# Hybrid backbone block: the first modulation with the weights stationary and two conditioning columns moving

## The chip, the cores and the metric

The kernel runs on one core of one Trainium2 chip. The time is that of the device, in microseconds, for one execution of the whole program. A run is compared by the median of several executions of the kernel before on the same chip.

## What is computed

One block of a flow-matching generator: 2048 latent tokens and 256 context tokens of width 1024. Everything is modulated by a vector computed from the conditioning `c` (for latent tokens) and `c_ctx` (for context tokens). The part that matters here:

```python
mod = jax.nn.silu(c) @ w_ada[l] + b_ada[l]          # 1024 -> 6 * 1024
mod_c = jax.nn.silu(c_ctx) @ w_ada[l] + b_ada[l]
sh1, sc1, g1, sh2, sc2, g2 = ...                     # six parts of 1024 each
q_c, k_c, v_c, p_c, gt_c = _split_proj(_modulate(ctx, csh1, csc1) @ w_in[l])
q, k, v, p, gt = _split_proj(_modulate(x, sh1, sc1) @ w_in[l])
```

`_modulate(z, shift, scale)` is the normalised z times (1 + scale) plus shift. After that come windowed attention with context keys, a pooling branch, gates, an output projection, a layer norm and a two-layer MLP. Only the first two parts of the modulation (shift and scale of the first sub-layer, 2048 of the 6144 columns of `w_ada`) are needed for both `c` and `c_ctx`, and they are needed first. The other four parts are computed much later in the program by another routine, on VectorE.

## The kernel before, in words

All products are made at the precision of float32. A plain float32 matmul of this kernel appears in the trace as two records of a matmul, each with a weight load of its own. The large products instead split each operand into a high and a low part (`split`, L57 to 62) and use three matmuls.

**The start.** The first 92 us or so are one stage, written as straight code (L127 to 400), whose order on each engine is set when the program is built by a scheduler with a model of the time line. From L401 on, the attention's order on TensorE is written out by hand.

**The first modulation.** The vector silu(c), silu(c_ctx) is built on ScalarE and VectorE as `cs`, 128 partitions x 8 k-tiles x 2 columns (L202 to 206). `csw` (L207, L208) widens it: each of the two columns is repeated 64 times, so that one k-tile of it is a full 128x128 stationary operand. `ada_load(c)` (L146) loads 512 columns of `w_ada` as four tiles `adaw` of 512 KB, two k-tiles each, and `ada_use(c, ws)` (L156) computes with them. There are four such chunks: 0 and 1 are the shift, 2 and 3 the scale; 0 and 2 serve the first half of the width, 1 and 3 the second. In `ada_use` eight float32 matmuls with `csw` as the stationary operand and 512 moving columns of weights make one PSUM bank `ps_ada` (L159), whose rows are 64 copies of either result. ScalarE copies it to `row` (L161), four transposes through TensorE bring the 512 columns onto partitions (`ps_adat`, L164), and VectorE picks one of the 64 copies, adds the bias and writes `mod` (L166); for chunks 2 and 3 it adds 1 (L168). `ps_ada` has the tag `proj`, of which there is one bank: the next chunk's first matmul waits until that bank has been read. The same bank later holds the q products.

**What follows in the start.** Two context blocks (xc) and two latent blocks (x01) are normalised on VectorE (L214), transposed (`ps_u`, L230), scaled by `mod` (L235 on ScalarE, L237 on VectorE), split (L240, L247) and multiplied by the k and v columns of `w_in` (`ps_ckv`, `ps_kv`, L252 to 254): the first half of the width after chunks 0 and 2, the second half after chunks 1 and 3. `wq_load(k)` (L176) loads the q columns, 8 times 512 KB through two buffers `wraw` (L179), and splits each on ScalarE (high) and on GpSimd (low; VectorE for the last two). `q_units` multiplies the blocks by them (`ps_q`).

**Buffers and queues.** The tiles `adaw`, `csw` and `wq` share two rings, a0 and a1, of eight buffers each, taken in program order: `csw` is the seventh tile of a0, the first `wq` the eighth. All DMAs shown here are issued by SyncE, in order. `row` shares a ring of four buffers with `ct`, `sg` and the q results.

Of the kernel before, what the change touches and what calls it, by code (L numbers as in the profile page):

```python
# [10 lines left out]
F32 = mybir.dt.float32  # L11
# [5 lines left out]
P = 128  # L17
D = 1024
T = 2048
KT = D // P  # L20
NB = T // P
CTX = 256
HD = 64
# [13 lines left out]
def block_kernel(  # L37
# [5 lines left out]
    pe, act, dve, pool, sp = nc.tensor, nc.scalar, nc.vector, nc.gpsimd, nc.sync  # L43
# [10 lines left out]
    def sbuf(name, side="left"):  # L54
        return tc.tile_pool(name=name, bufs=1, side=side, reuse_waits="tile")
# [16 lines left out]
    ident = const.tile([P, P], F32, name="ident")  # L72
# [6 lines left out]
    cs = const.tile([P, KT, 2], F32, name="cs")  # L79
# [24 lines left out]
    big = p1.enter_context(sbuf("p1big"))  # L104
# [6 lines left out]
    RA = (rp, "a", 8)  # L111
# [4 lines left out]
    def slot(where, i, shape, dt, name):  # L116
        pl, tag, n = where
        return pl.tile(shape, dt, name=name, tag=f"{tag}{i}", bufs=n)

    def ps512(name, tag="misc", bufs=1):  # L120
        return psb.tile([P, 512], F32, name=name, tag=tag, bufs=bufs)
# [15 lines left out]
    start = ExitStack()  # L137
# [17 lines left out]

    def ada_use(c, ws):  # L156
        ps = ps512("ps_ada", "proj")
        for k in range(KT):
            pe.matmul(ps, csw[:, k, :, :].rearrange("p a b -> p (a b)"), ws[k // 2][:, k % 2, :], start=k == 0, stop=k == KT - 1)  # L159
        row = big.tile([P, 512], F32, name="row", tag="q", bufs=4)  # L160
        act.copy(row, ps)  # L161
        pt = ps512("ps_adat")
        for i in range(4):
            pe.transpose(pt[:, i * P:(i + 1) * P], row[:, i * P:(i + 1) * P], ident)  # L164
        v = pt.rearrange("p (i c r) -> p i c r", i=4, c=2)[:, :, :, 0]
        dve.tensor_tensor(mod[:, 4 * c:4 * c + 4, :], v, badat[:, 4 * c:4 * c + 4].unsqueeze(2).broadcast_to([P, 4, 2]), ALU.add)  # L166
        if c in (2, 3):
            dve.tensor_scalar(mod[:, 4 * c:4 * c + 4, :], mod[:, 4 * c:4 * c + 4, :], 1.0, None, ALU.add)  # L168
# [35 lines left out]
    dve.tensor_scalar(sg, sg, 1.0, None, ALU.add)  # L204
    dve.reciprocal(sg, sg)
    dve.tensor_tensor(cs, ct, sg, ALU.mult)
    csw = slot(RA, 0, [P, KT, 2, HD], F32, "csw")  # L207
    dve.tensor_copy(csw, cs.unsqueeze(3).broadcast_to([P, KT, 2, HD]))  # L208
    dve.tensor_scalar(nsink, sinkt, -1.0, None, ALU.mult)


# [167 lines left out]
    for c in (0, 2):  # L379
        ada_use(c, ada_w[c])  # L380
# [3 lines left out]
    for c in (1, 3):  # L384
        ada_use(c, ada_w[c])
# [227 lines left out]
    for n, (b, g) in enumerate(order):  # L613
# [4 lines left out]
        for tok in (PLAN[g] if b + 2 < NB else TPLAN).split():  # L618
            t, i = tok[0], int(tok[1:] or 0)
# [41 lines left out]
    def ps2(name, tag="b", bufs=6):  # L661
        return pp.tile([P, 512], F32, name=name, tag=tag, bufs=bufs)
# [62 lines left out]
    for c in range(2):  # L725
# [100 lines left out]
        for n in range(4):  # L826
            w = wcols(w_in, 2048 + n * 256)
            for jj in range(2):
                ps = [ps2("ps_ga") for _ in HALF]
# [21 lines left out]
        for n in range(4):  # L851
            w = wcols(w_ab, n * 256) if n else w_first
            for jj in range(2):
                j = 2 * n + jj
                ps = [ps2("ps_ab") for _ in HALF]
# [356 lines left out]
    for name, v in (("g2", g2_scr), ("ln2g", ln2_g), ("ln2b", ln2_b)):  # L1212
        r = m2p.tile([P, D], F32, name=name)
# [140 lines left out]
```

## Time and profile before

| what | value |
|---|---|
| median of 3 runs | 3024.92 us (3024.32 to 3026.61) |
| the profiled execution's own time | 3021.76 us |
| its span, from the first to the last instruction | 3020.0 us |
| TensorE matmuls busy | 2899.2 us, 96% of the span |
| mean granted TensorE clock | 0.984 of full speed |
| VectorE, ScalarE, GpSimd busy | 60%, 45%, 46% |

The profiled execution lies 3.2 us under the median of the runs. A line of the profile names the engine (PE is TensorE's matmul, PEld its weight load, DVE VectorE, ACT ScalarE, POOL GpSimd, SPq the DMA issues of SyncE), the source line, the tile written and the tiles read, and the shapes. "128*128 128x512" is a stationary operand of 128x128 and a moving one of 512 columns. Matmul records overlap: the distance from start to start is the time that one costs, the duration holds the way through the array as well.

### The profile page before, as it was taken

The numbers are of one execution on the slowest core, as the hardware profiler recorded it, in microseconds if no ns is written. First come the engines' busy times: TensorE is split into PE (matmuls) and PEld (weight loads), VectorE is DVE, ScalarE is ACT, GpSimd is POOL, SyncE is SP. The second block draws the span as 40 slices with busy tenths as digits, with TensorE's granted clock in tenths as the row PEclk, the third lists the DMA queues.
The fourth block names the chain that finished last, engine by engine and source line by source line (L and its number), as shares of the span: only waits on it lengthen the run. The fifth ranks groups of instructions, "written<-read, shape, count | busy, mean of one in ns | idle before, by whom it ended". The sixth has DMA issues, their size and how long they took to land.

```text
span 3020.0 us, 42577 instructions
## 1 busy us (share of the span) xinstructions
PE 2899.2 (96%) x15336; PEld 2473.6 (82%) x15336; DVE 1817.9 (60%) x3201; ACT 1365.8 (45%) x2462; POOL 1382.5 (46%) x1638
## 2 busy tenths in 40 slices
PE   8899999999899999999999769999999989999998
PEld 5789989998888888888889758888888768888886
DVE  5578787877875444742144765558555453556675
ACT  4577777777751222332221455556555432233342
POOL 2867777777540014323033457666665340123244
PEclk9999999999999999999999889999999999999999
DMA  7111111112234433352132376547555684566663
GB/s 257 36 30 37 33 37 31 43 37 61 68 100 145 128 126 102 109 158 79 42 112 84 115 257 188 152 141 233 172 151 155 236 308 141 188 213 215 203 205 109
DMA packets 342663, 395.38 MB, mean 131 GB/s; under 512 B 16689, under 2 KB 276913, under 8 KB 340402
## 3 DMA queue, kind: packets, MB, share of 16 engines
q1 hardware_dynamic: 342450, 392.64, 40.8%
q8 instruction: 121, 1.98, 0.3%
q14 instruction: 92, 0.75, 0.1%
HBM read 275.13 MB, written 117.44 MB: 130 GB/s over the span
## 4 chain that ended last, share of the span: by engine, by line
PE 80%; DVE 7%; DMA 5%; POOL 3%; issue 3%; ACT 2%; SPq 0%; POOLq 0%; ACTq 0%; DVEq 0%
PE ps_h L1039 18%; PE ps_y L1254 16%; PE ps_o L503 4%; PE ps_pt L486 4%; PE ps_s L450 3%; PE ps_gp L688 2%; PE ps_ga L685 2%; PE ps_ga L688 2%; PE ps_ga L686 2%; PE ps_ab L685 2%; PE ps_ab L686 2%; PE ps_gp L685 2%; PE ps_ab L688 2%; PE ps_gp L686 2%; PE ps_s L451 2%
## 5 line engine op out<-in xcount | busy, mean ns | idle before, releaser
L1254 PE MATMUL ps_y<-La,R 128*128 128x512 f32 x2688 | 614.9, 391 | 15.5 <-ACT La L59 11.6
L1254 PEld LDWEIGHTS ps_y<-La,R 128*128 128x128 f32 x2688 | 506.5, 189 | 123.7 <-ACT La L59 12.8
L1039 PE MATMUL ps_h<-La,R 128*128 128x512 f32 x2112 | 488.4, 391 | 25.4 <-ACT La L59 22.1
L1039 PEld LDWEIGHTS ps_h<-La,R 128*128 128x128 f32 x2112 | 398.3, 189 | 110.3 <-ACT La L59 22.3
L62 DVE TENSOR_TENSOR R<-hraw,R 128x512 fp32r<-128x512 f32 x216 | 188.6, 883 | 153.9 <-ACT R L59 153.5
L62 DVE TENSOR_TENSOR pl<-ps_pt,ph 128x512 fp32r<-128x512 f32 x312 | 212.3, 685 | 70.6 <-ACT ph L59 68.6
L59 ACT CAST R<-hraw 128x512 fp32r<-128x512 f32 x216 | 131.9, 621 | 271.6 <-PE ps_y L1254 254.3
L465 POOL TENSOR_SCALAR s<-s,sm 128x640 f32<-128x640 f32 (+1 forms) x256 | 201.4, 796 | 102.1 <-DVE sm L464 53.8
L462 ACT ACTIVATE s<-s,sm 128x641 f32<-128x641 f32 (+1 forms) x256 | 209.9, 820 | 69.7 <-DVE sm L456 69.2
L861 POOL TENSOR_TENSOR sa<-sa,m 128x512 f32<-128x512 f32 x32 | 57.2, 1809 | 375.6 <-DVE sa L860 375.6
L456 DVE CUSTOM_DVE_ANT_0 s<-ps_s,mask,nsink 128x640 f32<-128x640 f32 (+1 forms) x256 | 211.3, 862 | 29.3 <-PE ps_s L451 29.0
L59 ACT CAST ph<-ps_pt 128x512 fp32r<-128x512 f32 x312 | 179.5, 580 | 108.5 <-PE ps_pt L486 105.3
L486 PE MATMUL ps_pt<-ident,s 128*128 128x128 f32 x1248 | 189.6, 274 | 12.2 <-DVE pl L62 7.8
L59 ACT CAST wh<-raw 128x2048 fp32r<-128x2048 f32 (+1 forms) x38 | 67.0, 1771 | 277.9 <-DMA raw<-w_in 75.7
L62 DVE TENSOR_TENSOR R<-sraw,R 128x512 fp32r<-128x512 f32 x160 | 147.0, 921 | 75.6 <-ACT R L59 75.2
L486 PEld LDWEIGHTS ps_pt<-ident,s 128*128 128x128 f32 x1248 | 151.3, 141 | 43.4 <-DVE pl L62 13.3
L62 DVE TENSOR_TENSOR wl<-raw,wh 128x2048 fp32r<-128x2048 f32 (+1 forms) x38 | 86.3, 2273 | 159.9 <-ACT wh L59 159.8
L59 ACT CAST R<-sraw 128x512 fp32r<-128x512 f32 x160 | 98.9, 621 | 153.1 <-PE ps_h L1039 95.2
L66 PE MATMUL ps_out<-wh,mg 128*128 128x256 f32 x512 | 143.1, 281 | 0.0
L67 PE MATMUL ps_out<-wl,mg 128*128 128x256 f32 x512 | 142.8, 280 | 0.0
L68 PE MATMUL ps_out<-wh,mg 128*128 128x256 f32 x512 | 142.6, 280 | 0.0
L1039 PE MATMUL ps_h<-Lb,R 128*128 128x512 f32 x576 | 136.1, 389 | 1.0 <-DVE cv L1057 1.0
(266 smaller groups left out, 7066.8 us busy)
## 6 DMA issues: line engine op xcount, KB each, us to landing
hraw<-hs_scr SPq DMA_DIRECT2D x108, 512.0 KB, 3.6
sraw<-w_mlp_in SPq DMA_DIRECT2D x64, 512.0 KB, 6.3
w<-w_mlp_out SPq DMA_DIRECT2D x64, 512.0 KB, 5.1
hs_scr<-s SPq DMA_DIRECT2D x96, 256.0 KB, 4.9
raw<-w_in SPq DMA_DIRECT2D x19, 1024.0 KB, 5.5
raw<-w_ada SPq DMA_DIRECT2D x16, 1024.0 KB, 5.2
rw<-us_scr SPq DMA_DIRECT2D x14, 1024.0 KB, 5.6
raw<-u_scr SPq DMA_DIRECT2D x8, 1032.0 KB, 5.9
```

Source lines behind the costliest of these rows:

```text
L59: act.copy(hi, src)
L62: (lo_eng or dve).tensor_tensor(lo, src, hi.bitcast(F32), ALU.subtract)
L66: pe.matmul(ps, sh, mh, start=first, stop=False)
L456: dve.tensor_tensor_reduce(out=s[:, 0:n], in0=pieces[z][2], in1=mk[z], op0=ALU.add, op1=ALU.min, scale=-1.0 / math.sqrt(HD), scalar=nsink[ ...
L462: act.activation(s[:, 0:n + 1], s[:, 0:n + 1], AF.Exp, bias=sm[:, 0, j:j + 1], scale=-1.0, accum_out=sm[:, 1, j:j + 1])
L465: pool.tensor_scalar(s[:, 0:n], s[:, 0:n], sm[:, 2, j:j + 1], 1.0, ALU.mult, ALU.mult)
L486: pe.transpose(pt[:, c:c + P], self.s.probs[2 * z + j][:, o:o + P], ident)
L685: pe.matmul(ps, wh[:, k, c:c + P], mh, start=k == 0, stop=False)
L686: pe.matmul(ps, wh[:, k, c:c + P], ml, start=False, stop=False)
L688: pe.matmul(ps, wl[:, k, c:c + P], mh, start=False, stop=k == KT - 1)
L1039: pe.matmul(ps, a, b, start=p in (1, 6, 5) and k == 0 and i == 0, stop=k == 3 and i == 2, skip_group_check=p not in (1, 6, 5))
L1254: pe.matmul(ps, a, b, start=n == 0 and z == 0, stop=n == 15 and z == 2)
```

## The change

`csw` is gone. For each 128 of a chunk's 512 columns (i, the outer loop) and each k-tile (k, the inner loop) the 128x128 block of `w_ada` itself is the stationary operand and the two columns of `cs` move. The result has the columns on partitions at once: eight numbers per partition in the bank `ps_ada`, from which VectorE adds the bias directly. The row copy on ScalarE, the tile `row`, the transposes and the bank `ps_adat` are gone. All loads are the same.

```diff
     def ada_use(c, ws):
         ps = ps512("ps_ada", "proj")
-        for k in range(KT):
-            pe.matmul(ps, csw[:, k, :, :].rearrange("p a b -> p (a b)"), ws[k // 2][:, k % 2, :], start=k == 0, stop=k == KT - 1)
-        row = big.tile([P, 512], F32, name="row", tag="q", bufs=4)
-        act.copy(row, ps)
-        pt = ps512("ps_adat")
         for i in range(4):
-            pe.transpose(pt[:, i * P:(i + 1) * P], row[:, i * P:(i + 1) * P], ident)
-        v = pt.rearrange("p (i c r) -> p i c r", i=4, c=2)[:, :, :, 0]
+            for k in range(KT):
+                pe.matmul(ps[:, 2 * i:2 * i + 2], ws[k // 2][:, k % 2, i * P:(i + 1) * P], cs[:, k, :],
+                          start=k == 0, stop=k == KT - 1)
+        v = ps[:, 0:8].rearrange("p (i c) -> p i c", c=2)
         dve.tensor_tensor(mod[:, 4 * c:4 * c + 4, :], v, badat[:, 4 * c:4 * c + 4].unsqueeze(2).broadcast_to([P, 4, 2]), ALU.add)
...
     dve.tensor_tensor(cs, ct, sg, ALU.mult)
-    csw = slot(RA, 0, [P, KT, 2, HD], F32, "csw")
-    dve.tensor_copy(csw, cs.unsqueeze(3).broadcast_to([P, KT, 2, HD]))
     dve.tensor_scalar(nsink, sinkt, -1.0, None, ALU.mult)
```

## Rows read from the trace of the kernel before

**Rows 1.** Busy time by stretch, whole span: PE, PEld, DVE, ACT, POOL, clock, DMA, GB/s.
```profile
0.00:45.00 45.00, 37.49 (x111) 19.26 (x112) 22.65 (x62) 15.03 (x30) 0.22 (x5) 1.00 0.93 335
45.00:92.00 47.00, 40.16 (x192) 31.31 (x191) 21.19 (x41) 20.22 (x38) 31.75 (x47) 1.00 0.30 98
92.00:740.00 648.00, 637.75 (x4315) 578.28 (x4314) 509.72 (x1208) 456.86 (x978) 490.15 (x954) 1.00 0.14 36
```
**Rows 2.** PE's time line in the start: start us, length us, instruction.
```profile
5.29 9.00 PE L159 MATMUL ps_ada<-adaw,csw 128*128 128x512 f32 x16 [5.29 <-DMA adaw<-w_ada]
15.77 1.38 PE L230 MATMUL ps_u<-ident,xt 128*128 128x128 f32 x8 [1.48 <-DVE xt L214]
17.42 7.03 PE L159 MATMUL ps_ada<-adaw,csw 128*128 128x512 f32 x16
25.13 0.66 PE L164 MATMUL ps_adat<-ident,row 128*128 128x128 f32 x4 [0.68 <-ACT row L161]
25.62 7.03 PE L159 MATMUL ps_ada<-adaw,csw 128*128 128x512 f32 x16
33.28 0.48 PE L252 MATMUL ps_ckv<-wkh,uh 128*128 128x512 f32 x1
...
37.56 0.60 PE L164 MATMUL ps_adat<-ident,row 128*128 128x128 f32 x4
38.00 7.03 PE L159 MATMUL ps_ada<-adaw,csw 128*128 128x512 f32 x16
44.47 0.80 PE L252 MATMUL ps_ckv<-wkh,uh 128*128 128x512 f32 x1
```
**Rows 3.** What PE waited for in 0 to 90 us: total us, times, longest us.
```profile
PE ps_q L253 <- POOL wq L62: 1.8, 1, 1.8
...
PE ps_ckv L254 <- DVE ul L247: 1.5, 1, 1.5
...
PE ps_kt L292 <- DVE kcl L62: 0.9, 1, 0.9
PE ps_ckv L252 <- ACT uh L240: 0.9, 1, 0.9
```
**Rows 4.** PEld's time line in the first chunk.
```profile
7.98 0.34 PEld L159 LDWEIGHTS ps_ada<-adaw,csw 128*128 128x128 f32 x1 [0.52 <-issue]
8.84 0.33 PEld L159 LDWEIGHTS ps_ada<-adaw,csw 128*128 128x128 f32 x1 [0.52 <-issue]
9.41 0.19 PEld L159 LDWEIGHTS ps_ada<-adaw,csw 128*128 128x128 f32 x1 [0.24 <-issue]
9.84 0.19 PEld L159 LDWEIGHTS ps_ada<-adaw,csw 128*128 128x128 f32 x1 [0.24 <-issue]
```
**Rows 5.** Time line of a two-column float32 product later in the kernel, PE, then PEld.
```profile
944.72 0.50 PE L719 MATMUL ps_ar<-ones,adacc 128*128 128x2 f32 x4
945.08 0.48 PE L685 MATMUL ps_gp<-uh,wh 128*128 128x512 f32 x1
...
944.72 0.41 PEld L719 LDWEIGHTS ps_ar<-ones,adacc 128*128 128x128 f32 x3
945.05 0.19 PEld L685 LDWEIGHTS ps_gp<-uh,wh 128*128 128x128 f32 x1
```
**Rows 6.** Time line of transposes, at 97 us and at 1731 us.
```profile
97.52 1.03 PE L486 MATMUL ps_pt<-ident,s 128*128 128x128 f32 x8
98.31 0.47 PE L252 MATMUL ps_q<-wq,uh 128*128 128x512 f32 x1
...
1731.70 3.53 PE L929 MATMUL ps_u<-ident,xn 128*128 128x128 f32 x14 [0.66 <-ACT u2f L930]
```
**Rows 7.** Busy time by stretch, columns as in rows 1.
```profile
770.50:773.90 3.40, 1.32 (x10) 1.32 (x11) 3.40 (x7) 3.20 (x8) 0.62 (x1) 0.97 0.25 49
773.90:777.40 3.50, 3.44 (x17) 3.03 (x16) 3.36 (x8) 0.01 (x1) 1.17 (x3) 0.54 0.95 315
...
1733.10:1736.50 3.40, 3.37 (x15) 2.29 (x13) 0.00 (x0) 2.87 (x4) 3.32 (x6) 0.53 0.70 194
1736.50:1739.90 3.40, 0.69 (x5) 0.42 (x4) 0.00 (x0) 1.45 (x2) 3.40 (x6) 0.97 1.00 308
```
**Rows 8.** DMA issues: the fourth tile of chunk 0, issued at 2.67 us; us to landing.
```profile
adaw<-w_ada SPq DMA_DIRECT2D x1, 512.0 KB, 6.8
```
**Rows 9.** DVE's time line before and at chunk 0's bias, and at chunk 3's.
```profile
18.84 1.29 DVE L88 BATCH_NORM_STATS2 st<-xt 128x6 f32<-128x512 f32 x2 [2.40 <-DMA xt<-x]
...
21.49 0.15 DVE L166 TENSOR_TENSOR mod<-ps_adat,badat 128x8 f32<-128x8 f32 x1
...
50.64 0.17 DVE L166 TENSOR_TENSOR mod<-ps_adat,badat 128x8 f32<-128x8 f32 x1 [8.70 <-PE ps_adat L164]
```
**Rows 10.** The chain that ended last, pieces between 40 and 78 us: start, length, what.
```profile
40.35 3.48 DMA wraw<-w_in
...
67.64 4.00 DMA wraw<-w_in
71.65 1.05 ACT wq L59
...
77.93 0.63 PE ps_kt L292 x4
```
**Rows 11.** Groups by line in 0 to 90 us.
```profile
L62 POOL TENSOR_TENSOR wq<-wraw,wq 128x1024 fp32r<-128x1024 f32 x6 | 14.4, 2401 | 49.8 <-ACT wq L59 49.8
...
L164 PE MATMUL ps_adat<-ident,row 128*128 128x128 f32 x16 | 2.5, 276 | 0.7 <-ACT row L161 0.7
...
L161 ACT COPY row<-ps_ada 128x512 f32<-128x512 f32 x4 | 2.3, 584 | 3.9 <-PE ps_ada L159 3.9
...
L208 DVE COPY csw<-cs 128x1024 f32<-128x1024 f32 x1 | 0.7, 693 | 0.0
```

## The prediction

> **What bounds the kernel now.** I read the busy time by stretch first. From 92 us on TensorE works nearly without a break (637.75 of 648 us in the attention [rows 1]), so what the start loses or gains on TensorE is carried to the end one for one, unless the start itself has room. The start is read next, from PE's time line [rows 2]: four chunks of the modulation, 16 records each, at 5.29, 17.42, 25.62 and 38.00 us, with the work on the first context and latent blocks between them. From 15.77 us on PE is hardly ever idle; between 45 and 78 us its waits add up to 5.1 us (1.8 + 1.5 + 0.9 + 0.9) [rows 3]. Against this stands the chain of waits, which does not name the modulation at all: between 40 and 72 us it runs through the loads of the q weights and their splits, and it reaches TensorE only at 77.93 us [rows 10]. So two lines run side by side up to about 78 us, the q weights and TensorE, and TensorE's has about 5 us of room. A gain on TensorE alone is worth little; a loss of more than 5 us comes out at the end.
>
> **The cost of a chunk.** Before: 16 records in 7.03 us, 0.43 us from one to the next [rows 2], set by the 512 moving columns. After: 4 x 8 matmuls, each two records, so 64 records with a weight load each and two moving columns; what paces them is the load. The kernel has this very shape later on: four records with two columns fill 944.72 to 945.08 us, and three of their loads, started at 944.72, make room for the next load at 945.05, so 0.11 us each [rows 5]. Eight transposes in a row, each with its own load, go from 97.52 to 98.31 us, 0.10 us each [rows 6]. At that pace a chunk costs 64 x 0.11 = 7.0 us: **at the full clock the exchange is even.**
>
> **The clock decides.** In the first chunk the loads start 0.86 us apart up to 8.84 us and 0.43 us apart from 9.41 us on, and one lasts 0.34 us first and 0.19 us then [rows 4]. That is the half and the full clock (1.2 and 2.4 GHz); the granted clock printed for the first 9 us is 1.00 and does not show it, the doubled distance does. At the half clock 14 transposes take 3.53 us, about 0.24 us each with the tail off [rows 6], twice the 0.10 to 0.11. So I price a new record at 0.22 us at the half clock, between 0.11 (if the load kept its pace) and 0.25; a chunk is then 64 x 0.22 = 14.1 us.
>
> Which clock will it be? No row shows a long run of loads with only two columns behind each; the two-column records of the kernel stand inside dense work. Near rows: in 770.5 to 773.9 us PE was at work for 1.32 of 3.4 us, and in the next stretch the mean clock is 0.54 [rows 7]; between 1731.70 and 1736.5 us PE did transposes of 128 columns back to back at the half clock, and behind them the clock is 0.97 [rows 6, 7]. So dense work stood before a rise and thin work before a fall. A new chunk moves 64 x 2 = 128 columns where the old one moved 16 x 512; of these rows the thin stretch is the nearest to it, and I take the half clock, from the first record on.
>
> The Trainium skill, TensorE: Matmul & The Clock Gate, section "Why this matters for your kernels", says that keeping TensorE continuously busy releases the full clock. If a gapless row of loads is "busy" in that sense the chunk is even and the time is that of the first rival below; no run here shows which it is.
>
> **The sum, part by part, against the 45.0 us at which chunk 3 ends now.**
> - Chunk 0. The loop over i is outside, so the group i = 0 needs all four tiles; the last lands at 2.67 + 6.8 = 9.5 us [rows 8]. Behind it stand 52 of the 64 records: 52 x 0.22 = 11.4, end at 20.9 us instead of 14.3.
> - The 8 transposes of the first two blocks at 0.24: 1.9, to 22.8 us (0.9 us at the full clock now).
> - Chunks 2 and 1: 14.1 each, to 51.0 us. Their loads have long landed.
> - 8 transposes more (1.9) and the 18 matmuls on the context block. These take 4.3 us now (33.28 to 37.56 [rows 2]); at the start dense work ran at the half clock from 5.29 to 9.41 us [rows 2, 4], so I add 2: to 59.2 us.
> - Chunk 3 begins at the full clock and loses it: between 7.0 and 14.1, I take the middle, 10.6: to 69.8 us. The dense work after it pays another 2.
> - Removed: 16 transposes, 4 x 0.4 = 1.7 us on PE [rows 2, 11]; three groups lie before 45.0, and are already left out above; the fourth takes 0.4 off.
>
> Delay: 69.8 - 45.0 + 2 - 0.4 = 26.4 us. Of PE's 5.1 us of room [rows 3] I take 3 as absorbed: the q weights come up in the meantime (1.8) and part of the rest. **Net +23 us.** The q weights do not turn into a second delay: their low parts from the fifth on reuse buffers of chunk 3, free at 69.8 us; the four splits left then, up to 2.4 us each [rows 11], with two more loads of 4 us [rows 10], end about 18 us later, and PE has 28 us of work to do in that time (45 to 78 us now, less its 5.1 us of waits).
>
> **Costed at nothing.** The row copies (4 x 0.58 us on ACT [rows 11]): ACT waits for DMA around them; their place in the chain before `mod` counts only in the first rival. The copy to `csw` (0.69 us [rows 11]) is not what the first matmul waits for; that is the first tile's landing [rows 2]. The ring a0 loses a tile, so each q weight's high part takes a buffer freed earlier; DMA issues are the same in number and order. A new wait: the bank `ps_ada` is now freed by VectorE's bias and no longer by ScalarE. VectorE did chunk 0's bias at 21.49 us, behind statistics that waited for a load up to 18.84 us [rows 9]; if it kept that place, chunk 2 would start at 21.6 us instead of 17.42, 4.2 us late. At the half clock chunk 0 ends at 20.9 us anyway, so the wait is hidden under 1 us; at the full clock it is a price of 0 to 4.2 us.
>
> From the profiled execution 3021.76 + 23 = 3045; the median of the runs lies 3.2 higher, and the forecast goes by it: **3024.9 + 23 = 3048 us.** Its own range: low with chunk 3 at the full clock, all 5.1 us absorbed and no second rise, 26.4 - 3.6 - 5.1 - 2 = +16; high with 0.25 per record (some 230 records, +7), chunk 3 at the half clock (+3.6) and nothing absorbed, +37. So 3040 to 3061.
>
> **Rivals.**
> 1. *The full clock holds, or the load keeps its 0.11 us.* For it: PE has no gap, and PEld would be busier than now. Against: rows 4, where the load's length fell with the clock, and rows 7. Chunk 0 ends at 9.5 + 52 x 0.11 = 15.2 us, 0.9 later; chunks 2, 1 and 3 are even; 1.7 us of transposes are gone; chunk 3's `mod`, now at 50.64 us [rows 9], comes some 5 us earlier because it no longer waits for a copy and a place between matmuls. But the q weights still end near 73 us [rows 10], so at most 3 us come through: -3 to +2 with the bank's wait, about 3023 us. The same page, section "LDWEIGHTS (loading the stationary operand)", gives a load's time by its columns alone, with no second figure for the slow clock; by it this rival would hold even at the half clock. The trace disagrees: 0.34 against 0.19 us [rows 4].
> 2. *Faster.* The mechanism is the earlier `mod`: it lets the second halves, and behind them SyncE's last q weight, start earlier, and all 5.1 us of waits and 1.7 us of transposes vanish: -6.8, 3018 us. It decides only if the clock is full and the last q weight (issued at 67.64 us [rows 10]) moves by as much. It needs both lines to shorten together.
> 3. *A mixed clock.* The transposes and context matmuls between the chunks bring the clock up for part of chunks 2 and 1 too; half of the loss then remains, +8 to +14, about 3035 us.
> That the matmuls do not come as written has no mechanism here: each needs its own weights. The scheduler may set another order; that moves work inside the start and not its sum.
>
> **Chances.** Forecast 0.58, mixed 0.12, rival 1 0.22, rival 2 0.08. A measurement of this kernel can tell about 0.2%, 6 us. The forecast and the mixed clock lie beyond it on the slow side (0.70), rival 1 within it (0.22), rival 2 beyond it on the fast side (0.08). The range leaves out rival 2 and the forecast's upper end: 3020 to 3058.
>
> **What would show it.** Right: granted clock near 0.5 in the stretches of the chunks, loads 0.22 us apart, a chunk near 14 us, chunk 3's last record near 70 us, and the transposes of k that stand at 77.93 us [rows 10] at about 101. Wrong: loads 0.11 us apart and chunks of 7 us (rival 1 or 2); chunk 0's bias late on VectorE with PE idle before chunk 2 (the bank); or a late modulation with the attention no later than now, which would mean more room than 5 us.

## The result, and the profile after

The kernel after takes 3046.14 us (median of 4 runs, 3041.86 to 3047.83) against 3024.62 us for the kernel before on the same chip (4 runs): 21.5 us slower, ratio 1.007 with a 95% interval of 1.0057 to 1.0082. The profiled execution took 3045.1 us with a span of 3043.3.

Where the time came in is seen from a few fixed points in the two traces. The first two fences are the views of one tile, each line with count, durations (min/median/max in ns) and the start of the first and last record in us: `ps_o` is the attention's output, `ps_out` the output projection, `ps_h` the first MLP product. Before:

```profile
L503 PE MATMUL ps_o<-ph,vring x368: 277/363/582, 105.0 to 863.8; 128*128 128x256 f32 x184
...
L66 PE MATMUL ps_out<-wh,mg x512: 274/280/366, 1178.4 to 1707.7; 128*128 128x256 f32 x171
...
L1039 PE MATMUL ps_h<-La,R x2112: 387/389/794, 1759.2 to 2372.0; 128*128 128x512 f32 x192
```

After:

```profile
L498 PE MATMUL ps_o<-ph,vring x368: 278/363/562, 125.4 to 884.3; 128*128 128x256 f32 x184
...
L66 PE MATMUL ps_out<-wh,mg x512: 274/280/366, 1198.9 to 1727.9; 128*128 128x256 f32 x171
...
L1034 PE MATMUL ps_h<-La,R x2112: 387/389/794, 1778.9 to 2392.2; 128*128 128x512 f32 x192
```

The attention begins 20.4 us later (125.4 against 105.0), and that distance hardly moves up to the end of the first MLP product (2392.2 against 2372.0, 20.2). So the loss is made in the start and carried whole. Now PE's time line of the start after, which answers to [rows 2]:

```profile
9.47 11.25 PE L160 MATMUL ps_ada<-cs,adaw 128*128 128x2 f32 x52 [0.42 <-DMA adaw<-w_ada]
20.58 1.95 PE L225 MATMUL ps_u<-ident,xt 128*128 128x128 f32 x8
22.32 13.65 PE L160 MATMUL ps_ada<-cs,adaw 128*128 128x2 f32 x64
36.23 5.71 PE L160 MATMUL ps_ada<-cs,adaw 128*128 128x2 f32 x26 [0.26 <-DVE mod L163]
41.80 1.95 PE L225 MATMUL ps_u<-ident,xt 128*128 128x128 f32 x8
43.54 8.11 PE L160 MATMUL ps_ada<-cs,adaw 128*128 128x2 f32 x38
51.51 0.77 PE L247 MATMUL ps_ckv<-wkh,uh 128*128 128x512 f32 x1
...
58.30 9.03 PE L160 MATMUL ps_ada<-cs,adaw 128*128 128x2 f32 x64
67.19 0.77 PE L248 MATMUL ps_ckv<-wkl,uh 128*128 128x512 f32 x1
```

Chunk 2 takes 13.65 us where it took 7.03, that is 0.213 us a record; chunk 3 begins at 58.30 and takes 9.03. It ends at 67.3 us where it ended at 45.0. The view of the tile `ps_ada` gives the loads' length:

```profile
L160 PEld LDWEIGHTS ps_ada<-cs,adaw x256: 188/333/338, 5.4 to 66.9; 128*128 128x128 f32 x128
```

The busy time by stretch gives the granted clock (columns as in [rows 1]):

```profile
22.50:35.90 13.40, 13.40 (x65) 13.38 (x63) 4.84 (x12) 1.40 (x4) 0.00 (x0) 1.00 1.02 366
...
58.30:63.50 5.20, 5.20 (x48) 5.20 (x47) 0.00 (x0) 1.04 (x1) 1.37 (x1) 0.99 0.55 189
63.60:67.00 3.40, 3.40 (x18) 3.40 (x18) 0.00 (x0) 1.04 (x1) 2.09 (x1) 0.50 0.00 0
67.20:70.30 3.10, 3.10 (x9) 2.48 (x10) 2.20 (x2) 0.00 (x0) 2.38 (x2) 0.52 0.55 165
```

The median load lasts 333 ns: the length of the half clock in [rows 4]. Chunk 3 shows both levels in one chunk: 48 records in 5.2 us at the full clock (0.11 us each), then a fall to the half clock, which lasts into the dense work behind it. The clock column says 1.00 for chunk 2 in spite of loads at the half pace; it did so for the first 9 us of the kernel before as well. The first change that this trace records comes only with the dense work on the context block: its matmuls start 0.43 us apart up to 56.35 us and 0.23 us apart from 56.67 us on, under the same 1.00. Before that point the column tells nothing, and the loads' length and distance do.

### The profile page after: what moved, and what is told of

The parts are those of the page before. It is cut to its first block, busy times and chain, and to the rows that moved or that the text cites. A ratio compares the mean times of both kernels' runs of the same rounds, so it can differ in the third digit from the quotient of the medians.

```text
span 3043.3 us, 42930 instructions
## 1 busy us (share of the span) xinstructions
PE 2926.7 (96%) x15512; PEld 2516.8 (83%) x15512; DVE 1818.3 (60%) x3200; ACT 1364.7 (45%) x2458; POOL 1379.5 (45%) x1638
## 5 line engine op out<-in xcount | busy, mean ns | idle before, releaser
L1034 PE MATMUL ps_h<-La,R 128*128 128x512 f32 x2112 | 488.3, 391 | 25.4 <-ACT La L59 21.5
L481 PEld LDWEIGHTS ps_pt<-ident,s 128*128 128x128 f32 x1248 | 151.0, 141 | 44.2 <-DVE pl L62 13.8
```

Of the source, the lines that this page charges most:

```text
L481: pe.transpose(pt[:, c:c + P], self.s.probs[2 * z + j][:, o:o + P], ident)
L1034: pe.matmul(ps, a, b, start=p in (1, 6, 5) and k == 0 and i == 0, stop=k == 3 and i == 2, skip_group_check=p not in (1, 6, 5))
```

## The experiments

The theory: a chunk of loads with two columns behind each runs at the half clock, and that alone makes the loss. Rivals: the loads cost 0.21 us in this form at any clock; the order (chunk 0's last tile, VectorE holding the bank) makes it; only the last chunk's lateness counts. "Narrow" stands for the new form with its two moving columns. Times are medians; the kernel before ran beside them on the same chip (3024.98 us over 22 runs for the first four kernels, 3024.42 over 23 for the others).

| kernel | us | ratio to before, 95% interval |
|---|---|---|
| 128 columns moving | 3026.25 | 1.0005 (0.9996 to 1.0014) |
| narrow in chunks 0 and 2 only | 3035.51 | 1.0032 (1.0019 to 1.0046) |
| narrow in chunks 1 and 3 only | 3038.16 | 1.0043 (1.0029 to 1.0056) |
| before, copy and transposes left out | 3023.15 | 0.9996 (0.9987 to 1.0005) |
| 128 columns, two banks | 3023.15 | 0.9993 (0.9984 to 1.0002) |
| left out, two banks | 3021.42 | 0.9984 (0.9975 to 0.9993) |
| before, chunk 3 twice | 3033.09 | 1.0028 (1.0018 to 1.0039) |
| 32 columns moving | 3047.87 | 1.0074 (1.0060 to 1.0088) |

### The same loads with 128 columns behind each

```diff
-                pe.matmul(ps[:, 2 * i:2 * i + 2], ws[k // 2][:, k % 2, i * P:(i + 1) * P], cs[:, k, :],
-                          start=k == 0, stop=k == KT - 1)
-        v = ps[:, 0:8].rearrange("p (i c) -> p i c", c=2)
+                pe.matmul(ps[:, i * P:(i + 1) * P], ws[k // 2][:, k % 2, i * P:(i + 1) * P],
+                          csw[:, k, :, :].rearrange("p a b -> p (a b)"), start=k == 0, stop=k == KT - 1)
+        v = ps.rearrange("p (i c r) -> p i c r", i=4, c=2)[:, :, :, 0]
```

(`csw` is built again as in the kernel before.)

> The changed order and all its 256 weight loads stay, but 128 columns move behind each load (each conditioning column 64 times) instead of 2. Clock theory (few moving columns let the clock stay at half, and that is the whole loss): loads 0.11 us apart and about 7 us for each chunk from the second on, so the kernel is back near the kernel before, 3019 to 3027 us. Rival, the loads themselves (in this form a load costs 0.21 us whatever moves behind it): chunks stay near 13.7 us and the time at 3046 us or above. Rival, the order (chunk 0 must wait for its last tile, and VectorE now frees the bank): chunks run in 7 us but start late, PE idle before them, and at least 5 us of the 21 remain, 3030 us or more.

Measured 3026.25 us. The loads in the view of the tile, and the busy time in the stretches of chunks 2 and 3:

```profile
L160 PEld LDWEIGHTS ps_ada<-csw,adaw x256: 187/192/339, 5.2 to 47.6; 128*128 128x128 f32 x128
```

```profile
20.10:27.30 7.20, 7.20 (x64) 7.13 (x64) 6.15 (x16) 2.88 (x6) 0.00 (x0) 1.00 1.06 397
40.80:47.90 7.10, 7.10 (x66) 7.10 (x65) 1.23 (x1) 2.34 (x3) 2.35 (x1) 1.00 0.54 161
```

The median load is back at 192 ns, a chunk at 7.1 us, and 20 of the 21.5 us are gone, with 256 loads in the same order. The rival of the loads falls, and so does the order as the cause of the loss. That a load can take 0.11 us with two columns behind it is seen in chunk 3 of the kernel after (48 records in 5.2 us). A little of the order is left in PE's time line: before chunk 2 PE waited for VectorE's bias.

```profile
20.01 7.41 PE L160 MATMUL ps_ada<-csw,adaw 128*128 128x128 f32 x64 [1.26 <-DVE mod L163]
```

### The new form in two chunks of four

```diff
         ps = ps512("ps_ada", "proj")
+        if c in (0, 2):
...
+        else:
...
```

The first branch holds the new form, the second the form before with copy and transposes; the other kernel of the pair has `c in (1, 3)`.

> Only chunks 0 and 2 in the new form, 1 and 3 as in the kernel before. Clock theory: chunk 0 ends at 20.6 us (6.3 late), chunk 2 at about 36 (11.5 late), chunk 1 begins at the half clock and loses some 2 us before the clock is up, so 13 us late on PE, less the 3 us that the start absorbed before: 3033 to 3037 us. Rival, only the last chunk counts (what follows waits for the last part of the modulation, not for PE's time): chunk 3 still in time by its own form, 3024 to 3028 us.

> Only chunks 1 and 3 in the new form, 0 and 2 as in the kernel before. Clock theory: chunk 1 begins at the full clock after chunk 2's dense matmuls and loses it on the way, 9 to 11 us instead of 7; chunk 3 likewise about 9; the dense work behind each pays about 2 us until the clock is up; 6 to 9 us on PE, of which 3 to 5 fit into the room: 3026 to 3031 us. Rival, only the last chunk counts: nearly the whole 21 us, 3038 us or more.

Measured 3035.51 and 3038.16 us, 10.5 and 13.2 slower. The first lies where the clock theory put it and 7.5 us above its rival's range: with chunks 1 and 3 in the old form, their lateness is that of PE. Its steps came as expected too: chunk 0 ends at 20.5 us and chunk 2 at 35.7, and chunk 1, in the old form, loses 2.2 us on the half clock that it finds:

```profile
36.00 9.26 PE L166 MATMUL ps_ada<-adaw,csw 128*128 128x512 f32 x16 [0.26 <-DVE mod L173]
```

The second missed the theory's range by 7 us and taken alone meets the rival's number; since the rival fails with the other half, I looked for what was sized wrong. The stretches of the second kernel, in order: chunk 2 (old form), chunk 1 in two parts, dense work, chunk 3 in two parts, dense work:

```profile
17.60:24.50 6.90, 6.90 (x17) 2.78 (x15) 5.46 (x16) 2.88 (x6) 0.00 (x0) 1.00 1.06 401
28.70:33.60 4.90, 4.90 (x24) 4.90 (x25) 1.60 (x5) 0.87 (x2) 0.00 (x0) 0.50 1.08 395
35.40:40.90 5.50, 5.50 (x28) 5.50 (x27) 3.88 (x9) 4.52 (x8) 0.00 (x0) 0.50 0.80 259
41.00:45.60 4.60, 4.60 (x12) 3.60 (x13) 0.72 (x2) 1.04 (x1) 0.24 (x1) 0.52 0.70 227
47.70:52.40 4.70, 4.70 (x44) 4.70 (x42) 0.00 (x0) 0.98 (x1) 2.37 (x2) 0.99 0.57 172
52.60:57.10 4.50, 4.50 (x23) 4.50 (x22) 0.00 (x0) 1.04 (x1) 3.81 (x2) 0.50 0.35 100
57.20:62.70 5.50, 5.50 (x14) 4.30 (x15) 0.73 (x2) 2.09 (x2) 3.11 (x2) 0.52 0.41 136
```

Here the clock column can be trusted, since the dense chunk's 16 records take 7.03 us under its 1.00. It says 0.50 in the narrow chunk behind that. Chunk 1 has waits for its tiles just before the fall; chunk 3 falls from 0.99 to 0.50 with PE and PEld busy throughout. Several sizes were off. Chunk 1 takes about 12.5 us of PE (25.72 to 40.9, less 1.7 for the transposes inside it and 0.9 of waits for its tiles), not 9 to 11. The 8 transposes inside it take 0.9 us more at the half clock than at the full one. The half clock outlasts the chunks by 4.6 and 5.5 us of dense work, half of which is lost: 2.3 and 2.8. So 5.5 + 0.9 + 0.9 + 2.3 for chunk 1 and 2.4 + 2.8 for chunk 3, less 0.8 for the transposes removed, make 14.0; at the first transposes behind chunk 3 PE is 13.8 us late (66.11 against 52.30). (Chunk 0 took 1.1 us longer in this execution; that went into the wait for the first blocks, and the next transposes start 0.1 us later.) And the 3 to 5 us of room were not there. The four waits of [rows 3] are gone, but behind 69.9 us a new one stands, and the clock is down behind it:

```profile
72.62 1.87 PE L237 MATMUL ps_u<-ident,xt 128*128 128x128 f32 x8 [2.70 <-DVE u L244]
```

```profile
72.80:76.20 3.40, 3.40 (x13) 3.01 (x13) 2.71 (x8) 2.34 (x7) 0.00 (x0) 0.50 0.22 37
```

The halves add up roughly: 10.5 + 13.2 = 23.7 against 21.5 for all four chunks.

### What the removed part was worth

```diff
-        row = big.tile([P, 512], F32, name="row", tag="q", bufs=4)
...
-            pe.transpose(pt[:, i * P:(i + 1) * P], row[:, i * P:(i + 1) * P], ident)
-        v = pt.rearrange("p (i c r) -> p i c r", i=4, c=2)[:, :, :, 0]
+        v = ps.rearrange("p (i c r) -> p i c r", i=4, c=2)[:, :, :, 0]
```

> The matmuls of the kernel before, but the row copy and the transposes are left out and the modulation is filled from the bank as it stands (other values, the same work after it). This is what the change removes, without what it adds. By the prediction's sum 1.7 us of PE and an earlier last part of the modulation, of which at most 3 us come through because the q weights end at the same time: 3021 to 3025 us. Rival 2 of the prediction (both lines shorten together): 3018 us or less.

This kernel leaves work out, so the modulation holds other values. Measured 3023.15 us; the interval holds no change. In the profiled execution, which took 3028.17 us and is the second longest of eleven, PE's time line shows what can stand against a gain:

```profile
20.38 10.17 PE L159 MATMUL ps_ada<-adaw,csw 128*128 128x512 f32 x16 [3.10 <-DVE mod L161]
```

The bank is freed by VectorE's bias, and that stands behind statistics that wait for a load, as in [rows 9]. PE idles 3.1 us before chunk 2, the clock falls in that time, and chunk 2 takes 10.2 us instead of 7.0. ScalarE's copy, which looks like pure overhead, had been freeing the bank early. In this execution the attention begins 3.8 us later than in the kernel before (108.8 against 105.0), while the median is 1.8 us under it; so the trace shows a price that one execution paid, and whether the others lost the clock there too is not shown. Two kernels let chunks 2 and 3 write the other bank, `misc`, where the transposes of the row had gone, one with the removed part still left out, one on the version with 128 columns:

```diff
-        ps = ps512("ps_ada", "proj")
+        ps = ps512("ps_ada", "proj" if c in (0, 1) else "misc")
```

> The matmuls of the kernel before, the row copy and the transposes left out (other values in the modulation), and chunks 2 and 3 in another bank than 0 and 1. With one bank the version without copy and transposes waited 3.1 us for VectorE before chunk 2, and chunk 2 then ran at the half clock (10.2 us instead of 7.0). If these 6 us are what hid the gain: 3017 to 3021 us. If the q weights set the end: not under 3021 us.

> The version with 128 moving columns, and chunks 2 and 3 write another bank than chunks 0 and 1 (the one that the transposes of the row used before), so that no chunk waits for VectorE's bias of the chunk just before. If that wait (1.5 us in the version with one bank, on a clock just up) is what ate the gain: 3020 to 3024 us, a little under the kernel before. If the q weights end at the same time and set the end of the start anyway: 3024 to 3027 us, as with one bank.

Measured 3021.42 (3.0 us under before by the medians; the interval, 2 to 8 us, excludes no change) and 3023.15 (1.3 under, the interval just holds no change). The first lies 0.4 us outside the range for the bank and inside the one for the q weights, which is finer than these runs can tell (3016.02 to 3024.10). Its profiled execution, 3016.55 us and among the shortest, waits for no bias any more, and yet the attention begins only 0.7 us earlier than in the kernel before (104.3 against 105.0). PE still waits for the q weights there:

```profile
PE ps_q L248 <- POOL wq L62: 1.9, 1, 1.9
```

So the copy and the transposes are worth some 3 us by the medians if the bank is not held; where these arise beyond the 0.7 us at the attention's start is not shown. The second lies in the range for the wait, but its interval overlaps that of the version with one bank, and in the traces its attention begins later (107.2 against 105.5); that the wait ate a gain is not shown. The version with 128 columns and two banks has neither the row copy nor the transposes; it is some 23 us faster than the kernel after and not to be told from the kernel before.

### The room in the start

```diff
-        for k in range(KT):
+        for k in [k for _ in range(2 if c == 3 else 1) for k in range(KT)]:
```

> The kernel before with chunk 3's eight matmuls done twice (the second time over the first, the same result): 7.0 us more of dense work on PE at the full clock, nothing else. The prediction's room of 3 to 5 us between 45 and 78 us: 2 to 4 us slower, 3026.5 to 3029 us. No room (PE's time comes out in full): 3031 to 3033 us.

Measured 3033.09 us, 8.7 slower, with an interval of 5.4 to 11.8: the 7.0 us added come out in full, and the 2 to 4 us that a room would leave are excluded. The profiled execution is the longest of seven (3039.45 us), but its attention begins 8.9 us later than in the kernel before (113.9 against 105.0), which is the median's loss; the rest of its length comes later and is not explained here:

```profile
L503 PE MATMUL ps_o<-ph,vring x368: 278/363/562, 113.9 to 873.8; 128*128 128x256 f32 x184
```

The longest of PE's waits in the first 90 us; ScalarE's time line around it; and the busy time in the stretches before, in and behind it:

```profile
PE ps_u L230 <- ACT u L235: 5.4, 1, 5.4
```

```profile
66.29 1.04 ACT L59 CAST wq<-wraw 128x1024 fp32r<-128x1024 f32 x1 [3.09 <-DMA wraw<-w_in]
67.24 1.50 ACT L235 ACTIVATE u<-ps_u,mod 128x128 f32<-128x128 f32 x4
```

```profile
58.00:63.00 5.00, 5.00 (x28) 4.14 (x27) 1.60 (x5) 1.91 (x2) 2.60 (x2) 1.00 0.34 116
63.50:68.70 5.20, 0.00 (x0) 0.00 (x0) 1.23 (x1) 2.41 (x6) 2.11 (x1) 0.81 0.62 199
68.80:73.80 5.00, 5.00 (x14) 4.09 (x15) 4.41 (x11) 2.63 (x4) 0.00 (x0) 0.52 0.50 153
```

The four short waits of [rows 3] are gone, and one of 5.4 us stands in their place: PE waits for a bank of transposes that ScalarE reads only at 67.24 us, since the split of q weights ahead of it waits 3.1 us for their load. In the idle time the clock falls, and the 5 us of dense work behind it go at the half pace. The room was no reserve that any delay can draw on. Other delays did find some: in the version with 128 columns chunk 3 ended 3.0 us late (48.0 against 45.0), and the attention began 0.5 us late (105.5 against 105.0). It depends on where the delay meets the other engines.

### An intermediate width

```diff
-    csw = slot(RA, 0, [P, KT, 2, HD], F32, "csw")
+    csw = slot(RA, 0, [P, KT, 2, 16], F32, "csw")
```

(and 32 columns of `ps` for each i, against the version with 128 columns.)

> As the version with 128 moving columns, with 32 of them (each conditioning column 16 times); the loads, 0.11 us apart at the full clock, still set the pace. If it behaves like 128 columns: 3023 to 3028 us, granted clock near 1 in chunks 2 and 1. If it behaves like two columns: 3043 to 3048 us, chunks near 13.7 us.

Measured 3047.87 us. The loads of the tile:

```profile
L160 PEld LDWEIGHTS ps_ada<-csw,adaw x256: 188/333/338, 5.2 to 69.0; 128*128 128x128 f32 x128
```

With 32 columns the kernel is as slow as with two, loads and all, as its second expectation had it; the version with 128 differs in nothing but the columns (and the width of `csw`). Why the clock stays down at 2 and 32 columns and is up at 128 no run here tells; the runs show that it does.

## Why the prediction was right

The forecast was 3048 us, the measurement 3046.14, and the mechanism is the one named: the chunks run at the half clock. That the number came within 2 us is partly luck. The sum put PE 23 us late behind the start, and the attention begins 20.4 us late; the errors behind that (chunk 3, the absorbed waits, new waits) cancel in part, and in the profiled pair 3 us more arise far behind the start. Point by point:

- **The exchange is even at the full clock.** Shown: chunk 3's first 48 records take 5.2 us at the full clock, 6.9 for 64; with 128 columns a chunk of 64 records takes 7.1 to 7.2 us, and the time is that of the kernel before.
- **The half clock in the chunks.** Shown by the loads' length, by chunk 3 of the kernel after and by the kernel with chunks 1 and 3 narrow. The row that the choice leaned on was a weak likeness: there PE was at work for 1.32 of 3.4 us [rows 7], and in the chunks it has no gap. Whether the one carries over to the other was open before the runs. The Trainium skill, TensorE: Matmul & The Clock Gate, section "Why this matters for your kernels", would have a continuously busy TensorE at the full clock. The trace disagrees: by its records PE is busy 13.40 of 13.40 us in 22.5 to 35.9 us and PEld 13.38, at half pace. The same page's "LDWEIGHTS (loading the stationary operand)" gives a load one time by its columns; here it is 333 ns with a distance of 0.213 us at the half clock and 192 ns with 0.11 us at the full one.
- **The sum.** Chunk 0's end: 20.9 forecast, 20.7 measured. Record at the half clock: 0.22, measured 0.213. Chunk 1's end with the transposes: 52.9, measured 51.5. Chunk 3: 10.6, measured 9.0. Its end: 69.8, measured 67.3. The dense work behind it: 2, measured 1.6 (half of 3.1 us, at a clock of 0.52).
- **The absorbed 3 us.** Right in size, wrong as an idea. All 5.1 us of PE's waits did vanish after chunk 3, so by the sum PE was 22.3 + 1.6 - 0.4 - 5.1 = 18.4 us late; by the attention's start it was 20.4. Between the two stand a new wait of 1.4 us for VectorE and another stretch at the half clock, together about 3 us:

```profile
105.94 0.66 PE L225 MATMUL ps_u<-ident,xt 128*128 128x128 f32 x4 [1.40 <-DVE krl L62]
108.15 1.03 PE L412 MATMUL ps_qt<-ident,qsb 128*64 128x128 f32 x4 [1.55 <-DVE u L232]
```

```profile
108.00:111.00 3.00, 2.85 (x9) 2.39 (x10) 0.69 (x1) 1.20 (x2) 2.75 (x5) 0.50 0.32 89
```

  (The wait of 1.55 us stands in the kernel before as well.)
  The kernel with chunk 3 done twice shows that this room is not there for any delay.
- **The price of regaining the clock.** 2 us behind a chunk were right in the full change and somewhat low in the kernel with chunks 1 and 3 (2.3 and 2.8). The fall in the middle of a chunk held for chunk 3 (9.0 and 9.4 us) and came earlier in chunk 1 of that kernel. In the full change that costs nothing, since there chunks 0, 2 and 1 never had the full clock to lose.
- **The bank held by VectorE.** Priced at under 1 us at the half clock (0.26 measured; 1.89 in the version with 32 columns, which is more) and 0 to 4.2 at the full one (1.26 with 128 columns; 3.1 with the copy left out, in an execution that lost 3.1 more because the clock fell). Right for the kernel after.
- **The sign to look for.** "Granted clock near 0.5 in the chunks" was wrong as a sign: the column says 1.00 there, for the reason told above. The other signs (loads 0.21 us apart, chunks near 14 us, the third group of transposes of k at 100.89 us instead of 77.93) came as written, and chunk 3's last record at 67 us for "near 70". The third group is the latest of its kind, though: the other three moved by 18.9 to 20.0 us, nearer to the attention's 20.4 than to the forecast's 23.
- **Rival 2.** It did not come to the test, since the clock was not full. With the removed part simply left out and the bank freed the median falls by 3.0 us and not by 6.8; the interval, 2 to 8 us, does not exclude 6.8, but the attention's start moved by 0.7.

What stays open: the last 3 us of the distance in the profiled pair arise after the first MLP product (the distance grows from 20.2 to 23.3 us in the span); single runs of either kernel differ by as much, and no run was spent on it.

## What to carry to other kernels

Before turning a product round so that few columns move, count its weight loads and ask what the clock will do while little else runs: here four times the records at a quarter of the distance were even, and the clock made the loss. At the full clock a record took 0.11 us with two moving columns and with 128, so a wider moving operand (128 repeated columns instead of two) took the loss back without a single load less. And look at what a removed copy was freeing: the copy of a bank on one engine kept the next chunk from waiting for another (3.1 us in the execution traced).

## What was not expected of the hardware

- With 32 columns moving behind each 128x128 load the kernel stood where it stood with two (3047.87 us, load median 333 ns); with 128 it was at the full clock (192 ns).
- The half clock outlasts the thin work: 4.6 and 5.5 us of dense matmuls behind the narrow chunks still ran at a mean clock of 0.52.
- Idle time of 3.1 us before a dense chunk cost another 3.1 us at the half clock in the execution traced (10.17 against 7.03 us).
- In the kernel after the clock column shows 1.00 until the first change is recorded, over 50 us at the half pace.
